# The first weights of a hybrid decoder layer in two parts of 256 columns, and half of x's first tile by ScalarE's queue

## The chip, the cores and the metric

The kernel runs on one core of a Trainium2 chip. The metric is the device time of one execution in microseconds (us). Before the change three runs took 457.81, 458.18 and 458.72 us; the median is 458.18.

A core has five engines with a queue of instructions each, and they work side by side: TensorE (PE in the profile; PEld is its weight load) for matmuls, VectorE (DVE) and ScalarE (ACT) for arithmetic on tiles, GpSimd (POOL), and SyncE (SP), which here issues most of the transfers from memory. ScalarE can issue transfers too, in the order of its own instructions. Engines wait for each other and for transfers by semaphores.

## The reference

One layer of a hybrid decoder: a normalised input goes through one wide projection; its columns feed a block-sparse attention, a gated linear recurrence and two merge gates. The part of it that matters here is the first:

```python
def rmsnorm(x, gain):
    xf = x.astype(jnp.float32)
    return xf * lax.rsqrt(jnp.mean(xf * xf, axis=-1, keepdims=True) + RMS_EPS) * gain.astype(jnp.float32)
...
    xn = rmsnorm(h, norm_gain[i]).astype(dt)
    proj = xn @ w_in[i]
    aq, ak, av, ag, bq, bf, bi, bg, gate_a, gate_b = jnp.split(proj, split_pts, axis=-1)
```

x is 512 tokens by 1024 features, `w_in` is 1024 by 6144, all in float32. `bi` (the recurrence's values) and `av` (the attention's values) are 512 columns each, and are the first two projections that the kernel computes.

## The kernel before

Every float32 product is made of three matmuls in a faster type, `fp32r`. Both operands are split into a high part (a copy in the narrower type) and a low part (the rest): `gh`, `gl` for x times its gain, `wh`, `wl` for a weight. Then high times high, low times high and high times low are summed in PSUM. For a tile of x the high part is made by ScalarE (`A.activation`, with the gain as scale) and the low part by VectorE. For weights it is the same, except the very first one, whose high part VectorE casts, since ScalarE is taken by x there.

x lies transposed: eight tiles `xr0` to `xr7` of 128 features by 512 tokens. The projections `bi` and `av` are computed with tokens in the partitions: four PSUM banks each, one for 128 tokens. `chunk(g, k, ts)` adds the product of feature tile k into the banks `ts` of `bi` (g = 2) or `av` (g = 3): for each of the three products one matmul of 512 columns per bank. The factor of the norm (one number per token) is put on later, so that these matmuls can start before the sum of squares is known.

The order of instructions on ScalarE, VectorE and SyncE in this first stretch, and on TensorE throughout, is the order in which the code calls them. It begins so:

- TensorE runs eight matmuls on constants (`warm`, L156) while the first data come.
- SyncE issues, in this order: the left half of `xr0` (tokens 0 to 255), the first half of the first weights `wf0` (128 features by 512 columns, 256 KB), the right half of `xr0`, the first half of `wf1` (for `av`), `xr1`, and the second halves of `wf0` and `wf1` (L283 to L289). ScalarE's queue brings only `sm`, the small vectors with the gain (L141, 9 KB).
- `w_halves(0)` and `w_halves(1)` are generators that split the weights half by half, one step at each `next`. The first step casts the first half of `wf0` on VectorE (L312).
- Then x's left half is scaled and split (L205, L206), `chunk(2, 0, (0, 1))` multiplies it for the token banks 0 and 1, x's right half is scaled and split, and `chunk(2, 0, (2, 3))` follows. Then come `chunk(3, 0)` with `wf1`, and so on with the next tiles of x.
- A one-element `memset` on VectorE (L852) holds the transfer of `xr2` back until VectorE has come that far.

Of the kernel before, what the change touches and what calls it, by code (L numbers as in the profile page):

```python
# [11 lines left out]
F32 = mybir.dt.float32  # L12
R = mybir.dt.float32r
I32 = mybir.dt.int32
AF = mybir.ActivationFunctionType
OP = mybir.AluOpType
# [44 lines left out]
def hybrid_layer_kernel(  # L61
# [15 lines left out]
    nc = tc.nc  # L77
    V, A, G, PE = nc.vector, nc.scalar, nc.gpsimd, nc.tensor
# [11 lines left out]
    def unit(tag, name, dt=F32, shape=(128, 512)):  # L90
        return sb.tile(list(shape), dt, tag=tag, bufs=BUFS[tag], name=name)

    def bank(tag, name):
        return psum.tile([128, 512], F32, tag=tag, bufs={"mm": 4, "g": 2, "a": 2}[tag], name=name)
# [15 lines left out]
    def spawn(gen, after=0.0):  # L110
        sides.append([now[0] + after, gen])

    def run_due():
        again = True
        while again:
            again = False
            for s_ in list(sides):
                w = s_[0]
                if callable(w):
                    if not w():  # L120
                        continue
                elif w > now[0]:
                    continue
                again = True
                try:
                    y = next(s_[1])
                    s_[0] = y if callable(y) else now[0] + y
                except StopIteration:
                    sides.remove(s_)

    def tick(us):
        now[0] += us
        run_due()
# [3 lines left out]


    sm = cst.tile([128, NSMALL], F32, name="sm")
    with tc.high_priority():  # L140
        nc.scalar.dma_start(sm, smalls)  # L141
    A.preload_act_table_set("natural_log_exp_and_others")
    mkf = cst.tile([128, 32 + 32 * 7], F32, name="mkf")
    xr = []

    def load_x(k0, k1):
        for k in range(k0, k1):
            t = unit("H", f"xr{k}")
            nc.sync.dma_start(t, xT[:, k, :])
            xr.append(t)  # L150
# [18 lines left out]
    gain = sm[:, 0:8]  # L169
# [9 lines left out]
    def lower_bound():  # L179
        V.tensor_scalar(qgain, sm[:, 8:9], 0.125, None, op0=OP.mult)  # L180
        V.tensor_copy(lb[:, 0], lbl)
        V.tensor_sub(lb[:, 1], lbl, lb[:, 0])
        A.activation(lb[:, 1], lb[:, 1], AF.Exp)
        V.reciprocal(lb[:, 2], lb[:, 1])
        V.tensor_mul(lb[:, 2], lb[:, 1], lb[:, 2])
        V.tensor_sub(lb[:, 3], lb[:, 2], lb[:, 2])
        V.tensor_scalar(lb[:, 4], lb[:, 3], -1.0, 1.0, op0=OP.mult, op1=OP.add)
        A.activation(lb[:, 5], lb[:, 4], AF.Ln)
# [11 lines left out]
    def split(hi, lo, src):  # L200
        A.activation(hi, src, AF.Copy)
        V.tensor_tensor(lo, src, hi.bitcast(F32), op=OP.subtract)

    def scale_split(hi, lo, src, g):
        A.activation(hi, src, AF.Copy, scale=g)  # L205
        V.scalar_tensor_tensor(lo, src, g, hi.bitcast(F32), op0=OP.mult, op1=OP.subtract)  # L206

    wseq, wraw, wtile, wpos = [], [], [], [0]
# [19 lines left out]
    def w_load(upto):  # L228
        while len(wraw) <= min(upto, len(wseq) - 1):
            ap, kn, cols = wseq[len(wraw)]  # L230
            raw = unit("w", f"wf{len(wraw)}", shape=(128, kn, cols))
            nc.sync.dma_start(raw, ap)
            wraw.append(raw)

    def w_split(upto):
        while len(wtile) <= min(upto, len(wseq) - 1):
            i = len(wtile)
            w_load(i)
            ap, kn, cols = wseq[i]
            hi = unit("wh", f"wh{i}", R, (128, kn, cols))  # L240
            lo = unit("wl", f"wl{i}", R, (128, kn, cols))
            with tc.high_priority(offset=AHEAD):
                A.activation(hi, wraw[i], AF.Copy)  # L243
                pin(V.tensor_tensor(lo, wraw[i], hi.bitcast(F32), op=OP.subtract))  # L244
            wtile.append((hi, lo))
# [31 lines left out]


    with tc.high_priority():
        x0 = unit("H", "xr0")  # L280
        xr.append(x0)
        wraw.extend(unit("w", f"wf{i}", shape=(128, 2, 512)) for i in range(2))
        nc.sync.dma_start(x0[:, 0:256], xT[:, 0, 0:256])  # L283
        nc.sync.dma_start(wraw[0][:, 0], wseq[0][0][:, 0])
        nc.sync.dma_start(x0[:, 256:512], xT[:, 0, 256:512])
        nc.sync.dma_start(wraw[1][:, 0], wseq[1][0][:, 0])
        load_x(1, 2)
        for i in range(2):
            nc.sync.dma_start(wraw[i][:, 1], wseq[i][0][:, 1])  # L289


    gh, gl, xh, xl = [], [], [], []
# [3 lines left out]
    def x_gain(k0, k1):  # L296
        for k in range(k0, k1):
            h_ = unit("A", f"gh{k}", R)
            l_ = unit("A", f"gl{k}", R)
            scale_split(h_, l_, xr[k], gain[:, k:k + 1])  # L300
            gh.append(h_)
            gl.append(l_)

    def w_halves(i):

        hi = unit("wh", f"wh{i}", R, (128, 2, 512))
        lo = unit("wl", f"wl{i}", R, (128, 2, 512))
        wtile.append((hi, lo))
        for kk in range(2):
            if i == 0 and kk == 0:  # L310

                V.tensor_copy(hi[:, kk], wraw[i][:, kk])  # L312
                yield
                V.tensor_tensor(lo[:, kk], wraw[i][:, kk], hi[:, kk].bitcast(F32), op=OP.subtract)
            else:
                split(hi[:, kk], lo[:, kk], wraw[i][:, kk])
            yield
# [3 lines left out]
    def x_square(k):  # L321
        if k == 0:
            A.activation(ssum, xr[0], AF.Square)
            return
        t = unit("YB", f"xsq{k}")
        A.activation(t, xr[k], AF.Square)
        V.tensor_tensor(ssum, ssum, t, op=OP.add)
# [21 lines left out]
    def x_norm():  # L349
        with tc.high_priority(offset=AHEAD):  # L350
            y, rstd = column_norms(ssum, D, "xn", "YB")
            for g in range(4):
                V.tensor_copy(rt[32 * g:32 * g + 32], y[0:32].rearrange("p (t g) -> p t g", g=4)[:, :, g])
            x_normalise(rstd)
        done.add("rt")
        yield RT
# [468 lines left out]

    tok = {2: [bank("mm", f"bi{t}") for t in range(NT)], 3: [bank("ga"[t // 2], f"av{t}") for t in range(NT)]}

    def chunk(g, k, ts=range(NT)):

        wh, wl = wtile[PAIRED.index((g, k // 2))]  # L830
        for x_, w_, i in ((gh, wh, 0), (gl, wh, 1), (gh, wl, 2)):
            for t in ts:
                PE.matmul(tok[g][t], x_[k][:, t * 128:t * 128 + 128], w_[:, k % 2, :], start=(k == 0 and i == 0),  # L833
                          stop=(k == KD - 1 and i == 2))
            tick(0.227 * len(ts))
# [3 lines left out]
    with tc.manual_schedule(engines=FIRST):  # L839
        h_ = unit("A", "gh0", R)  # L840
        l_ = unit("A", "gl0", R)
        gh.append(h_)
        gl.append(l_)
        w0, w1 = w_halves(0), w_halves(1)
        next(w0)
        scale_split(h_[:, 0:256], l_[:, 0:256], xr[0][:, 0:256], gain[:, 0:1])
        next(w0)
        chunk(2, 0, (0, 1))
        scale_split(h_[:, 256:512], l_[:, 256:512], xr[0][:, 256:512], gain[:, 0:1])
        chunk(2, 0, (2, 3))  # L850
        t = unit("H", "xr2")
        V.memset(t[:, 0:1], 0.0)  # L852
        nc.sync.dma_start(t, xT[:, 2, :])
        xr.append(t)
        load_x(3, 4)
        next(w1)
        chunk(3, 0)
        x_gain(1, 2)
        next(w0)
        chunk(2, 1)  # L860
        w_load(2)
        load_x(4, 5)
        next(w1)
        chunk(3, 1)
        w_load(3)
        load_x(5, KD)
        x_square(0)
        x_square(1)
        x_gain(2, 3)
        w_split(2)  # L870
        x_gain(3, 4)
        chunk(2, 2)
        chunk(2, 3)
        x_square(2)
        w_load(4)
        w_split(3)
        x_square(3)
        x_gain(4, 5)
        x_square(4)
        w_load(5)  # L880
        chunk(3, 2)
        x_gain(5, 6)
        x_square(5)
        chunk(3, 3)
        x_square(6)
        x_gain(6, 7)
        x_square(7)
        w_split(4)
        x_gain(7, KD)
        lower_bound()  # L890
        nc.sync.dma_start(mkf, masks)
        wpos[0] = 4
        spawn(x_norm())
# [48 lines left out]
    for n in range(KD):  # L942
# [3 lines left out]
        h_ = unit("YB", f"mh{n}", R)  # L946
        l_ = unit("A", f"ml{n}", R)
# [140 lines left out]
    for at, n in enumerate(PAIRS):  # L1088
# [24 lines left out]
        if at in (2, 3):  # L1113
            t = unit("A", f"pf{at}")
# [201 lines left out]
```

## Time and profile before

| what | value |
|---|---|
| median of three runs | 458.18 us (457.81 to 458.72) |
| the profiled execution | 458.14 us |
| its span, first to last instruction | 456.1 us |
| TensorE busy | 450.5 us, 99% |
| VectorE busy | 338.7 us, 74% |
| ScalarE busy | 290.6 us, 64% |
| TensorE's granted clock over the span | 1.0 |
| bytes moved by DMA | 57.80 MB, 127 GB/s on average |

The span is counted from the first instruction to the last; the execution's own time is 2.0 us longer. In the profile `wf<-in_w_tok_dram` is a transfer of weights, `xr<-in_xT_dram` one of x; `wh`, `wl`, `gh` and `gl` are the split parts, and `bi` and `av` PSUM banks. In a timeline each line has the start and the length in us, the engine, the line of the kernel, the operation, what it writes and reads, and in brackets how long the engine stood idle before it and what ended that. SPq and ACTq are the issues of transfers on SyncE's and ScalarE's queues. A line of the view of waits has who waited for whom, then us in total, how many times, and the longest. In a group of instructions the numbers are us busy and mean ns of one.

### The profile page before, as it was taken

The numbers are of one execution on the slowest core, as the hardware profiler recorded it, in microseconds if no ns is written. First come the engines' busy times: TensorE is split into PE (matmuls) and PEld (weight loads), VectorE is DVE, ScalarE is ACT, GpSimd is POOL, SyncE is SP. The second block draws the span as 40 slices with busy tenths as digits, with TensorE's granted clock in tenths as the row PEclk, the third lists the DMA queues.
The fourth block names the chain that finished last, engine by engine and source line by source line (L and its number), as shares of the span: only waits on it lengthen the run. The fifth ranks groups of instructions, "written<-read, shape, count | busy, mean of one in ns | idle before, by whom it ended". The sixth has DMA issues, their size and how long they took to land.

```text
span 456.1 us, 7786 instructions
## 1 busy us (share of the span) xinstructions
PE 450.5 (99%) x2903; PEld 383.9 (84%) x2903; DVE 338.7 (74%) x718; ACT 290.6 (64%) x534; POOL 9.0 (2%) x32
## 2 busy tenths in 40 slices
PE   8999999999999999999999999999999999999996
PEld 7888888888888888888888888888888888899996
DVE  5789567869989778958798456414368878899885
ACT  5837555658688988889799487666224445457431
POOL 1000000010000010001000100000000000000000
PEclk9999999999999999999999999999999999999999
DMA  6742223342744344244424442224324534463112
GB/s 212 262 139 92 94 92 99 116 157 65 242 133 143 104 149 147 87 126 140 167 71 144 122 156 93 82 70 136 107 70 119 203 100 161 155 208 116 48 47 93
DMA packets 24358, 57.80 MB, mean 127 GB/s; under 512 B 2944, under 2 KB 5888, under 8 KB 24320
## 3 DMA queue, kind: packets, MB, share of 16 engines
q1 hardware_dynamic: 19568, 49.95, 34.5%
q10 hardware_dynamic: 4752, 7.35, 4.4%
q8 instruction: 23, 0.38, 0.3%
q14 instruction: 15, 0.12, 0.1%
HBM read 45.75 MB, written 2.10 MB: 105 GB/s over the span
## 4 chain that ended last, share of the span: by engine, by line
PE 98%; DMA 1%; DVE 0%; ACT 0%; issue 0%; SPq 0%; ACTq 0%; DVEq 0%
PE gb L260 10%; PE ga L260 10%; PE h L260 10%; PE ak L388 5%; PE ub L260 5%; PE bq L260 5%; PE bi L833 5%; PE bf L260 5%; PE ag L260 5%; PE aq L388 5%; PE bg L260 5%; PE av L833 5%; PE ua L260 5%; PE pe L1143 2%; PE gc L1152 2%; PE gd L1152 2%
## 5 line engine op out<-in xcount | busy, mean ns | idle before, releaser
L243 ACT ACTIVATE wh<-wf 128x1024 fp32r<-128x1024 f32 (+1 forms) x70 | 67.2, 960 | 66.9 <-PE ub L260 10.8
L244 DVE TENSOR_TENSOR wl<-wf,wh 128x1024 fp32r<-128x1024 f32 (+1 forms) x70 | 76.9, 1099 | 39.5 <-ACT wh L243 37.9
L260 PE MATMUL gb<-xh,wh 128*128 128x512 f32 x64 | 25.7, 402 | 0.0
L260 PE MATMUL ga<-xh,wh 128*128 128x512 f32 x64 | 25.2, 393 | 0.0
L260 PE MATMUL gb<-xh,wl 128*128 128x512 f32 x64 | 25.0, 391 | 0.0
L260 PE MATMUL ga<-xh,wl 128*128 128x512 f32 x64 | 25.0, 390 | 0.0
L260 PE MATMUL ga<-xl,wh 128*128 128x512 f32 x64 | 25.0, 390 | 0.0
L260 PE MATMUL gb<-xl,wh 128*128 128x512 f32 x64 | 25.0, 390 | 0.0
L260 PE MATMUL h<-ml,wh 128*128 128x512 f32 x64 | 24.9, 389 | 0.0
L260 PE MATMUL h<-mh,wl 128*128 128x512 f32 x64 | 24.9, 389 | 0.0
L260 PE MATMUL h<-mh,wh 128*128 128x512 f32 x64 | 24.9, 389 | 0.0
L708 ACT ACTIVATE p<-p,ps 128x128 f32<-128x128 f32 (+3 forms) x32 | 17.6, 552 | 5.5 <-DVE ps L706 5.5
L706 DVE CUSTOM_DVE_ANT_0 p<-s,bias 128x128 f32<-128x128 f32 (+3 forms) x32 | 14.2, 485 | 5.9 <-PE s L697 4.5
L718 ACT ACTIVATE p<-p,ps 128x128 f32<-128x128 f32 (+3 forms) x32 | 15.9, 552 | 0.5 <-DVE ps L716 0.5
L260 PEld LDWEIGHTS gb<-xh,wl 128*128 128x128 f32 x64 | 12.0, 188 | 2.6
L260 PEld LDWEIGHTS ga<-xh,wl 128*128 128x128 f32 x64 | 12.0, 188 | 2.6
L260 PEld LDWEIGHTS h<-mh,wh 128*128 128x128 f32 x64 | 12.0, 188 | 2.5
L260 PEld LDWEIGHTS h<-ml,wh 128*128 128x128 f32 x64 | 12.0, 188 | 2.5
L260 PEld LDWEIGHTS h<-mh,wl 128*128 128x128 f32 x64 | 12.0, 188 | 2.4
L260 PEld LDWEIGHTS ga<-xl,wh 128*128 128x128 f32 x64 | 12.0, 188 | 2.3
L260 PEld LDWEIGHTS ga<-xh,wh 128*128 128x128 f32 x64 | 12.0, 188 | 2.3
L260 PEld LDWEIGHTS gb<-xl,wh 128*128 128x128 f32 x64 | 12.0, 188 | 2.2
(408 smaller groups left out, 1368.5 us busy)
## 6 DMA issues: line engine op xcount, KB each, us to landing
wf<-in_w_tr_dram SPq DMA_DIRECT2D x32, 512.0 KB, 3.3
wf<-in_w_tok_dram SPq DMA_DIRECT2D x14, 512.0 KB, 3.3
wf<-in_w_up_dram SPq DMA_DIRECT2D x16, 256.0 KB, 2.7
wf<-in_w_o_dram SPq DMA_DIRECT2D x8, 512.0 KB, 3.3
pc<-p ACTq DMA_DIRECT2D x16, 192.0 KB, 2.2
bias<-in_brow_dram SPq DMA_DIRECT2D x8, 256.0 KB, 3.4
pc<-p ACTq DMA_DIRECT2D x8, 256.0 KB, 2.7
xres<-in_xT_dram SPq DMA_DIRECT2D x8, 256.0 KB, 3.0
```

What stands on the lines that cost most here:

```text
L243: A.activation(hi, wraw[i], AF.Copy)
L244: pin(V.tensor_tensor(lo, wraw[i], hi.bitcast(F32), op=OP.subtract))
L260: PE.matmul(ps, a[:, k, :], b[k], start=(n == 0), stop=(n == tot - 1))
L388: PE.matmul(banks[t], a[:, s_], b[:, kk, :], start=(k == 0 and i == 0), stop=(k == KD - 1 and i == 2))
L706: V.tensor_tensor_reduce(p_, sp[j][:, o:o + nk], T[2 * hp + j][:, nk - 1::-1], -1.0, 3e38, OP.add, OP.min, st[:, 0:1])
L708: A.activation(p_, p_, AF.Exp, bias=st[:, 0:1], scale=-1.0, accum_out=st[:, 1:2])
L718: A.activation(p_, p_, AF.Copy, scale=st[:, 2:3])
L833: PE.matmul(tok[g][t], x_[k][:, t * 128:t * 128 + 128], w_[:, k % 2, :], start=(k == 0 and i == 0), stop=(k == KD - 1 and i == 2))
L1143: PE.matmul(pes[i][:, cols], wt[:, i, k, :], t[k][:, cols], start=k == n == 0, stop=k == 1 and n == 2 and (bool(parts) or cols == right))
L1152: PE.matmul(dst[:, left], wt[:, k, :], bt, start=begin and n == 0, stop=n == 11, skip_group_check=not begin)
```

## The change

Three things change at the start of the program:

- x's right half is issued on ScalarE's queue, behind `sm`, instead of on SyncE's.
- The first half of `wf0` comes in two transfers of 256 columns. VectorE casts the left one, and ScalarE copies the right one into its high part. VectorE makes the two low parts one after the other.
- The products of token banks 0 and 1 with these weights are made by a new function, `first_chunk`, in matmuls of 256 columns: left columns and then right columns in each of the three products.

The steps of x's left half are written out, so that they stand between the steps of the weights. The rest of the program is the same.

```diff
+    x0 = unit("H", "xr0")
     with tc.high_priority():
         nc.scalar.dma_start(sm, smalls)
+        nc.scalar.dma_start(x0[:, 256:512], xT[:, 0, 256:512])
...
         nc.sync.dma_start(x0[:, 0:256], xT[:, 0, 0:256])
-        nc.sync.dma_start(wraw[0][:, 0], wseq[0][0][:, 0])
-        nc.sync.dma_start(x0[:, 256:512], xT[:, 0, 256:512])
+        for cols in (slice(0, 256), slice(256, 512)):
+            nc.sync.dma_start(wraw[0][:, 0, cols], wseq[0][0][:, 0, cols])
         nc.sync.dma_start(wraw[1][:, 0], wseq[1][0][:, 0])
...
             if i == 0 and kk == 0:
-
-                V.tensor_copy(hi[:, kk], wraw[i][:, kk])
+                l_, r_ = slice(0, 256), slice(256, 512)
+                V.tensor_copy(hi[:, kk, l_], wraw[i][:, kk, l_])
                 yield
-                V.tensor_tensor(lo[:, kk], wraw[i][:, kk], hi[:, kk].bitcast(F32), op=OP.subtract)
+                A.activation(hi[:, kk, r_], wraw[i][:, kk, r_], AF.Copy)
+                yield
+                for cols in (l_, r_):
+                    V.tensor_tensor(lo[:, kk, cols], wraw[i][:, kk, cols], hi[:, kk, cols].bitcast(F32), op=OP.subtract)
...
+    def first_chunk():
+
+        wh, wl = wtile[0]
+        for n, (x_, w_) in enumerate(((gh, wh), (gl, wh), (gh, wl))):
+            for cols in (slice(0, 256), slice(256, 512)):
+                for t in (0, 1):
+                    PE.matmul(tok[2][t][:, cols], x_[0][:, t * 128:t * 128 + 128], w_[:, 0, cols],
+                              start=(n == 0 and cols.start == 0), stop=False)
+        tick(0.227 * 6)
...
-        scale_split(h_[:, 0:256], l_[:, 0:256], xr[0][:, 0:256], gain[:, 0:1])
+        A.activation(h_[:, 0:256], xr[0][:, 0:256], AF.Copy, scale=gain[:, 0:1])
         next(w0)
-        chunk(2, 0, (0, 1))
+        V.scalar_tensor_tensor(l_[:, 0:256], xr[0][:, 0:256], gain[:, 0:1], h_[:, 0:256].bitcast(F32),
+                               op0=OP.mult, op1=OP.subtract)
+        next(w0)
+        first_chunk()
```

SyncE's queue at the start of the program, before the change and then after it (`xr0` is x's first tile, `wf0` and `wf1` the first two weights):

```order
L283 DMA xr0_94<-in_xT_dram 128x256
L284 DMA wf0_95<-in_w_tok_dram 128x512
L285 DMA xr0_94<-in_xT_dram 128x256
L286 DMA wf1_96<-in_w_tok_dram 128x512
L149 DMA xr1_101<-in_xT_dram 128x512
```

```order
L284 DMA xr0_67<-in_xT_dram 128x256
L286 DMA wf0_96<-in_w_tok_dram 128x256 x2
L287 DMA wf1_97<-in_w_tok_dram 128x512
L151 DMA xr1_102<-in_xT_dram 128x512
L290 DMA wf0_96<-in_w_tok_dram 128x512
```

Four transfers stand ahead of `xr1` in both (`x2` counts two). The 256 KB of `wf0` are now two of 128 KB, and x's second 128 KB are no longer among them.

ScalarE's queue at the same place, before and after (`gh0` is x's high part, `wh0` and `wh1` those of the weights):

```order
L141 DMA sm_66<-in_smalls_dram 128x18
L142 ACT_TABLE_LOAD
L205 ACTIVATE gh0_120<-xr0_94,sm_66 128x256 x2
L201 ACTIVATE wh1_147<-wf1_96 128x512
L205 ACTIVATE gh1_163<-xr1_101,sm_66 128x512
```

```order
L142 DMA sm_66<-in_smalls_dram 128x18
L143 DMA xr0_67<-in_xT_dram 128x256
L144 ACT_TABLE_LOAD
L860 ACTIVATE gh0_121<-xr0_67,sm_66 128x256
L315 ACTIVATE wh0_123<-wf0_96 128x256
L207 ACTIVATE gh0_121<-xr0_67,sm_66 128x256
L203 ACTIVATE wh1_156<-wf1_97 128x512
```

The issue of x's right half stands ahead of the table load, and the copy of the weights' right half stands between the two scalings of x.

TensorE's queue behind the warm matmuls, before and after (`bi0` and `bi1` are the banks of tokens 0 to 127 and 128 to 255, `bi2` the next):

```order
L833 MATMUL bi0_110<-wh0_122,gh0_120 128x512
L833 MATMUL bi1_111<-wh0_122,gh0_120 128x512
L833 MATMUL bi0_110<-wh0_122,gl0_121 128x512
L833 MATMUL bi1_111<-wh0_122,gl0_121 128x512
L833 MATMUL bi0_110<-wl0_123,gh0_120 128x512
L833 MATMUL bi1_111<-wl0_123,gh0_120 128x512
L833 MATMUL bi2_112<-wh0_122,gh0_120 128x512
```

```order
L838 MATMUL bi0_111<-wh0_123,gh0_121 128x256
L838 MATMUL bi1_112<-wh0_123,gh0_121 128x256
L838 MATMUL bi0_111<-wh0_123,gh0_121 128x256
L838 MATMUL bi1_112<-wh0_123,gh0_121 128x256
L838 MATMUL bi0_111<-wh0_123,gl0_122 128x256
L838 MATMUL bi1_112<-wh0_123,gl0_122 128x256
```

Six matmuls have become twelve of half the width; of these the first two read only the left columns of the weights, and the third and fourth the right ones.

More of the change, by code (lines that the diff above doesn't have):

```diff
@@ L279, in hybrid_layer_kernel @@
     with tc.high_priority():
-        x0 = unit("H", "xr0")
         xr.append(x0)
```

## The prediction

> **What bounds the kernel now.** I read the head of the page first, then the chain of work that ended last.
>
> ```profile
> span 456.1 us, 7786 instructions
> PE 450.5 (99%) x2903; PEld 383.9 (84%) x2903; DVE 338.7 (74%) x718; ACT 290.6 (64%) x534; POOL 9.0 (2%) x32
> PE 98%; DMA 1%; DVE 0%; ACT 0%; issue 0%; SPq 0%; ACTq 0%; DVEq 0%
> ```
>
> TensorE (PE) is busy for 99% of the span and makes 98% of the chain. No other engine can pay for a saved microsecond; only idle time of PE on that chain can. The view of waits, for PE alone over the whole span, shows how much of that there is:
>
> ```profile
> PE bi L833 <- DVE wh L312: 1.0, 1, 1.0
> PE warm L156 <- PEq L1303: 0.8, 1, 0.8
> PE ktp L670 <- ACT sc L548: 0.4, 1, 0.4
> ```
>
> Three waits. The 0.8 us is the program's start and the 0.4 us belongs to the attention; the change touches neither. What is left is one wait of 1.0 us, ahead of the first real matmul. The timeline around it, thinned to what matters:
>
> ```profile
> 0.73 0.39 SPq L283 DMA_DIRECT2D xr<-in_xT_dram  x1
> 0.74 0.41 ACTq L141 DMA_DIRECT2D sm<-in_smalls_dram  x1
> 1.18 0.42 SPq L284 DMA_DIRECT2D wf<-in_w_tok_dram  x1
> 1.19 1.28 ACT L142 ACT_TABLE_LOAD   x1 [1.19 <-PEq L1303]
> 1.65 0.42 SPq L285 DMA_DIRECT2D xr<-in_xT_dram  x1
> 2.11 0.43 SPq L286 DMA_DIRECT2D wf<-in_w_tok_dram  x1
> 3.23 0.51 ACT L205 ACTIVATE gh<-xr,sm 128x256 fp32r<-128x256 f32 x1 [0.76 <-DMA sm<-in_smalls_dram]
> 3.75 0.38 PE L156 MATMUL warm<-const-float32-1.0 128*128 128x128 f32 x2
> 4.53 0.43 DVE L312 CAST wh<-wf 128x512 fp32r<-128x512 f32 x1 [3.64 <-DMA wf<-in_w_tok_dram]
> 4.93 0.51 ACT L205 ACTIVATE gh<-xr,sm 128x256 fp32r<-128x256 f32 x1 [1.20 <-DMA xr<-in_xT_dram]
> 5.11 0.70 PE L833 MATMUL bi<-wh,gh 128*128 128x512 f32 x2 [0.98 <-DVE wh L312]
> 5.27 0.69 DVE L314 TENSOR_TENSOR wl<-wf,wh 128x512 fp32r<-128x512 f32 x1
> 6.44 0.63 ACT L201 ACTIVATE wh<-wf 128x512 fp32r<-128x512 f32 x1 [0.99 <-DMA wf<-in_w_tok_dram]
> 6.58 0.63 PE L833 MATMUL bi<-wh,gh 128*128 128x512 f32 x2
> 7.96 1.08 PE L833 MATMUL av<-wh,gh 128*128 128x512 f32 x4
> ```
>
> The warm matmuls end at 3.75 + 0.38 = 4.13. The first weights land, VectorE (DVE) casts them from 4.53 to 4.96, and PE starts at 5.11. x's left part and its scaling are done by 3.74, so the weights alone decide. From 5.11 on PE has work at every moment but that 0.4 us. So **the whole of what can be won is 5.11 - 4.13 = 0.98 us**, 0.21% of 458.14. The time can fall by over 0.2% (0.92 us, about what a measurement of this kernel can tell from no change) only if nearly all of it is won.
>
> When the transfers land, from the view of DMAs cut to the moment of each issue (last column: us from issue to landing):
>
> ```profile
> xr<-in_xT_dram SPq DMA_DIRECT2D x1, 128.0 KB, 2.3
> wf<-in_w_tok_dram SPq DMA_DIRECT2D x1, 256.0 KB, 3.3
> xr<-in_xT_dram SPq DMA_DIRECT2D x1, 128.0 KB, 3.3
> wf<-in_w_tok_dram SPq DMA_DIRECT2D x1, 256.0 KB, 4.3
> ```
>
> With the issue times above that is 3.03 for 128 KB in all, 4.48 for 384 KB, 4.95 for 512 KB and 6.41 for 768 KB. I use these four marks below: what SyncE's queue had brought by when.
>
> **The change part by part.** Two things move: x's right part (128 KB) goes from SyncE's queue to ScalarE's, and the first 256 KB of weights become two halves of 128 KB, the left cast by DVE and the right by ScalarE (ACT). SyncE still issues four transfers up to the second weights, so those are issued at 2.11 as before.
>
> *The left half* lands at a time L. Before it come x's left part and perhaps some of x's right part: between the 256 KB mark, which an even share of 3.03 to 4.48 puts at 3.75, and the 384 KB mark, 4.48. The cast of 256 columns has no row; half of the 0.43 above and all of it bound it, and I take 0.30. Pick-up (4.48 to 4.53) is 0.05 and cast to PE (4.96 to 5.11) is 0.15. PE starts at L + 0.50, from 4.25 to 4.98: 0.1 to 0.9 earlier. If that were all, the change would be a gain. But the left half feeds two matmuls, and the third needs the right half.
>
> *The right half* lands at R. ACT copies it; the nearest rows are a copy of this size, and the scaled one of the same size:
>
> ```profile
> L966 ACT ACTIVATE b11h<-hf 128x256 fp32r<-128x256 f32 x3 | 1.2, 402 | 0.0
> L205 ACT ACTIVATE gh<-xr,sm 128x256 fp32r<-128x256 f32 x2 | 1.0, 510 | 2.0 <-DMA xr<-in_xT_dram 1.2 <-DMA sm<-in_smalls_dram 0.8
> ```
>
> So 0.40 to 0.51; I take 0.41, the plain copy. ACT to PE has no row at such a place; I take DVE's 0.15, with 0.03 as the other end (ACT to DVE, 7.07 to 7.10). The third matmul starts at R + 0.05 + 0.41 + 0.15 = **R + 0.61**.
>
> *The matmuls.* Six of 512 columns become twelve of 256. From the stretch near the end of the kernel, where 24 matmuls of that size stand between these two:
>
> ```profile
> 405.07 0.29 PE L1152 MATMUL ga<-b11h,gwh 128*128 128x256 f32 x1
> 407.87 0.28 PE L1152 MATMUL gc<-tah,s1h 128*128 128x256 f32 x1
> ```
>
> 2.80 / 24 = 0.117 each, 1.40 for twelve, against 1.47 from 5.11 to 6.58 now (it includes a short wait for `wl`). Ten are left when the right half is ready, 1.17 us. **The next pair of tiles starts at R + 1.78, against 6.58 now. The change breaks even at R = 4.80.**
>
> *So what is R?* By then x's left part, both halves and some share of x's right part have come: at least 384 KB and at most 512 KB. The marks give 4.48 (-0.32 us) and 4.95 (+0.15 us). Nothing in the trace shows two queues loading from memory together: `sm` on ACT's queue is 9 KB. Since x's right part is issued at about 1.15, ahead of the right half (1.65), most of it should be in front; since it is behind `sm`, not all. I take R = 4.80, nearer the upper mark: **0.0 us**. PE's wait is then cut in two: it starts at about 4.6, does 0.23 us of work, and stands again until about 5.4.
>
> [...]
>
> *What hides the rest.* ACT issues one more DMA, 0.41 us, ahead of its table load, which then ends at about 2.88 instead of 2.47; the first ACTIVATE waits for `sm` until 3.23 anyway. Without that cover it would cost nothing until PE's 4.25. On ACT the wait for the right half now stands ahead of x's right scaling (0.51), which ends at R + 0.97 and is needed at R + 1.78; behind it ACT has the second weights at 6.44, later than both. On DVE the right `wl` is done at about R + 0.9 and needed at R + 1.55. Each margin is 0.6 to 0.8 us; past it each costs one for one.
>
> *Whether a gain would last.* The second weights' high part is ready at 6.44 + 0.63 + 0.15 = 7.22 against its use at 7.96: 0.74 of the 0.98 us passes, unless those weights come sooner too. After that:
>
> ```profile
> 12.59 1.06 ACT L243 ACTIVATE wh<-wf 128x1024 fp32r<-128x1024 f32 x1 [1.89 <-DMA wf<-in_w_tok_dram]
> 16.13 1.07 PE L833 MATMUL bi<-wh,gh 128*128 128x512 f32 x4
> 47.33 1.29 DVE L202 TENSOR_TENSOR xl<-xr,xh 128x512 fp32r<-128x512 f32 x2
> 48.77 0.39 PE L260 MATMUL bf<-xh,wh 128*128 128x512 f32 x1
> ```
>
> The third weights are ready at 13.65 for 16.13, and the last of `xl` at 48.62 for a use 21 matmuls behind 48.77. So whatever the start gains or loses, up to 0.74 us, goes to the end unchanged.
>
> **The rivals.** *Faster: R comes early.* The rate over 40 slices of 0.7 to 4.6 us:
>
> ```profile
> GB/s 0 0 0 0 0 0 0 0 0 0 21 95 126 127 192 265 271 297 284 282 341 420 399 420 273 200 179 147 126 137 105 126 95 74 105 158 221 158 189 168
> ```
>
> It reaches 420 near 3 us and sags to about 130 until past 4. Nothing I can name causes the sag. If two queues fill it, 384 KB behind the 3.03 mark at 400 GB/s take 0.98: R = 4.01, a gain of 0.79, of which 0.74 passes: 457.4. Against it: the sag falls when SyncE's queue already holds enough work. 25%.
>
> *Slower: the right half falls behind.* The marks at 512 and 768 KB are 1.46 us apart, so a late mark is as much in the trace as an early one. If the sag meets R, halfway between them, R = 5.68; PE stands in the middle of its first chunk with everything queued behind it, and loses 0.88: 459.0. It decides from R = 4.80 on, one for one. Against it: it needs more than the 512 KB to be served ahead. 10%.
>
> *The change does not do what it says:* x's right part is served ahead of the left half, L is 4.48 and R 4.95; PE starts 0.13 sooner, and the next pair 0.15 later: 458.3. 5%.
>
> **How the numbers follow.** The sum is made against the profiled execution: 458.14 us, of which 456.1 are its span and 2.0 lie around it. The median of the three runs, 458.18, is the same; they lie 0.91 apart. Forecast, no change, 60%: 458.1. Of the faster case's 25%, 8 end over 0.92 us faster with that scatter, and of the forecast's 60 about 2; of the slower case's 10%, 4 end over 0.92 us slower, and about 2 of the forecast's. Faster 10%, same 84%, slower 6%. The range runs from the faster case with a little scatter, 457.3, to just short of the slower case, 458.9.
>
> **What would show it.** In the profile after: PE's first real matmul between 4.25 and 5.0, then two matmuls of 256 columns, then a second wait whose releaser is ACT's `wh`. The twelve take 1.4 us without their wait. ACT's copy of the right half starts near 4.85 and takes 0.4. The pair of tiles 2 and 3 starts within 0.3 us of 6.58, and every later chunk keeps that shift. The prediction is wrong if the copy starts before 4.5 or after 5.2, or if a wait of PE stands anywhere later that was not there before.

## The result, and the profile after

The changed kernel takes 461.28 us (median of 21 runs, 458.73 to 463.21) against 458.37 us (457.40 to 459.04) for the kernel before in the same measurement. The ratio is **1.0061, 95% interval 1.0050 to 1.0071**: about 2.8 us slower. The prediction was 458.1 us, no change.

The runs of the changed kernel do not lie around one value: five are below 460 us and sixteen between 460.7 and 463.2.

The head of the page of the changed kernel, its chain, and the transfers of code, which are a queue of their own:

```profile
span 459.2 us, 7803 instructions
PE 453.4 (99%) x2909; PEld 386.4 (84%) x2909; DVE 338.8 (74%) x719; ACT 290.6 (63%) x535; POOL 10.0 (2%) x32
q8 instruction: 23, 0.38, 0.3%
PE 98%; DMA 1%; issue 0%; DVE 0%; SPq 0%; ACT 0%; DVEq 0%
```

PE still makes 98% of the chain, and it is busy 2.9 us longer, though it has only six matmul records more (2909 against 2903). The waits of PE over the whole span:

```profile
PE pt L741 <- issue: 0.8, 1, 0.8
PE warm L158 <- PEq L1320: 0.8, 1, 0.8
PE bi L838 <- ACT wh L315: 0.5, 1, 0.5
```

The wait of 1.0 us has become one of 0.5 us, so the start looks better. A wait at `pt` is new. Neither explains 3 us. The timeline of the start does:

```profile
1.18 0.89 SPq L286 DMA_DIRECT2D wf<-in_w_tok_dram  x2
1.18 0.44 ACTq L143 DMA_DIRECT2D xr<-in_xT_dram  x1
4.02 0.29 DVE L313 CAST wh<-wf 128x256 fp32r<-128x256 f32 x1 [3.13 <-DMA wf<-in_w_tok_dram]
4.46 0.77 PE L838 MATMUL bi<-wh,gh 128*128 128x256 f32 x2
5.25 0.42 ACT L315 ACTIVATE wh<-wf 128x256 fp32r<-128x256 f32 x1 [1.53 <-DMA wf<-in_w_tok_dram]
5.72 0.80 PE L838 MATMUL bi<-wh,gh 128*128 128x256 f32 x2 [0.49 <-ACT wh L315]
6.32 1.05 PE L838 MATMUL bi<-wh,gl 128*128 128x256 f32 x4
8.02 1.05 PE L847 MATMUL bi<-wh,gh 128*128 128x512 f32 x2
8.88 1.05 PE L847 MATMUL bi<-wh,gl 128*128 128x512 f32 x2
9.73 0.75 PE L847 MATMUL bi<-wl,gh 128*128 128x512 f32 x2
10.32 1.09 PE L847 MATMUL av<-wh,gh 128*128 128x512 f32 x4
11.25 1.08 PE L847 MATMUL av<-wh,gl 128*128 128x512 f32 x4
```

PE starts at 4.46 instead of 5.11 and is ahead. But read the distance from row to row: two matmuls of 512 columns take 8.88 - 8.02 = 0.86 us, 0.43 each; four take 11.25 - 10.32 = 0.93, 0.23 each. **TensorE runs at half rate until about 10 us.** In the kernel before it had full rate from its first real matmul on: the six from 6.58 to 7.96 in the prediction's rows take 0.23 us each. The trace also keeps a record of each change of the granted clock, with its time, and that says the same: full rate from 9.98 here, from 3.57 before. `av` starts at 10.32 against 7.96, so 2.36 of the span's 3.0 us are lost by then.

The right half came late too. The view of DMAs cut to the issues at 1.2 to 1.7 us (the right half of the weights is issued near 1.6):

```profile
xr<-in_xT_dram ACTq DMA_DIRECT2D x1, 128.0 KB, 3.7
wf<-in_w_tok_dram SPq DMA_DIRECT2D x1, 128.0 KB, 3.6
```

ScalarE takes the right half up at 5.25, so R was 5.20 where the prediction had 4.80.

### The profile page after: what moved, and what is told of

Same layout as the page of the kernel before. It is cut to its first block, busy times and chain, and to the rows that moved or that the text cites. A ratio compares the mean times of both kernels' runs of the same rounds, so it can differ in the third digit from the quotient of the medians.

```text
span 459.2 us, 7803 instructions
## 1 busy us (share of the span) xinstructions
PE 453.4 (99%) x2909; PEld 386.4 (84%) x2909; DVE 338.8 (74%) x719; ACT 290.6 (63%) x535; POOL 10.0 (2%) x32
## 4 chain that ended last, share of the span: by engine, by line
PE 98%; DMA 1%; issue 0%; DVE 0%; SPq 0%; ACT 0%; DVEq 0%
PE gb L262 10%; PE ga L262 10%; PE h L262 10%; PE ak L392 5%; PE ub L262 5%; PE bq L262 5%; PE bf L262 5%; PE ag L262 5%; PE aq L392 5%; PE bg L262 5%; PE av L847 5%; PE ua L262 5%; PE bi L847 5%; PE pe L1160 2%; PE gc L1169 2%; PE gd L1169 2%
```

## The experiments

Three causes had to be told apart: the clock, the late landing through the second queue, and something later in the program, where the wait at `pt` is. Ratios are to the kernel before, run beside each kernel on the same chip. The kernels were run in four sets, not all on one chip, so I compare medians only within a set, and otherwise the ratios.

**First set: fill the pauses, undo the queue, move the queue alone, lengthen the pause.**

Filling TensorE's pauses of the changed kernel:

```diff
-WARM = 8
+WARM = 9
...
             for cols in (slice(0, 256), slice(256, 512)):
+                if n == 0 and cols.start:
+                    for i in range(3):
+                        PE.matmul(tok[2][2][:, 0:128], one, one, start=True, stop=True)
                 for t in (0, 1):
```

> The changed kernel with one more warm matmul at the start and three matmuls on constants (into a bank that is overwritten later) in the wait between the second and the third real matmul: the pauses of TensorE are filled, nothing else moves. Clock theory: what the change costs is mostly TensorE at half rate until about 10 us (512 columns in 0.43 us instead of 0.23), because the two pauses keep it from full speed; filled, full rate comes before 7 us and the time is 457.9 to 459.0 us, ratio 0.999 to 1.001. Landing theory: the right half of the weights and its copy on ScalarE come late and the delay is passed on; filling does nothing, the time stays at 460.5 to 461.5 us, ratio 1.005 to 1.007.

Measured 460.05 us, ratio 1.0039 (1.0027 to 1.0052): between the two. The trace shows why. The copy of the right half started at 5.14, nearly as late as in the changed kernel, but the rate was full:

```profile
5.61 0.51 PE L841 MATMUL bi<-wh,gh 128*128 128x256 f32 x2
5.96 0.64 PE L841 MATMUL bi<-wh,gl 128*128 128x256 f32 x4
6.43 0.64 PE L841 MATMUL bi<-wl,gh 128*128 128x256 f32 x4
6.91 0.63 PE L850 MATMUL bi<-wh,gh 128*128 128x512 f32 x2
```

Four matmuls of 256 columns in 0.47 us, and the next pair at 6.91, 0.33 late instead of 1.44 (8.02). With full rate most of the loss at the start is gone. The trace alone does not show that filling brought it: its clock record has full rate from 4.04, ahead of the filled wait. The times say more: all five runs lie between 459.90 and 461.02, where sixteen of the changed kernel's twenty-one were over 460.7, although this kernel loses 1.2 us between 200 and 260 us, 0.9 more than the changed one. Neither theory had that. In its waits there is a new 1.1 us, and two lines of the timeline show it between dense small matmuls:

```profile
253.31 0.46 PE L541 MATMUL lpa<-hq,hk 128*32 128x48 f32 x24
254.83 0.29 PE L541 MATMUL lpa<-hq,hk 128*32 128x48 f32 x8 [1.06 <-issue]
```

PE waited for nothing that the profile shows ("issue"), in the middle of a series. I come back to it.

x's right half back on SyncE's queue, the split kept:

```diff
-        nc.scalar.dma_start(x0[:, 256:512], xT[:, 0, 256:512])
...
+        nc.sync.dma_start(x0[:, 256:512], xT[:, 0, 256:512])
         nc.sync.dma_start(wraw[1][:, 0], wseq[1][0][:, 0])
```

> The changed kernel with x's right half back on SyncE's queue, behind both halves of the weights: only the queue move is undone. Landing theory: the right half lands at the 384 KB mark, near 4.5 us, the copy on ScalarE starts near 4.5 instead of 5.25, and the time is at or a little below before, ratio 0.999 to 1.000. [...]

Measured 458.85 us, ratio 1.0007 (0.9998 to 1.0015). The timeline of its PE:

```profile
4.18 1.10 PE L838 MATMUL bi<-wh,gh 128*128 128x256 f32 x4
5.12 0.64 PE L838 MATMUL bi<-wh,gl 128*128 128x256 f32 x4
5.59 0.64 PE L838 MATMUL bi<-wl,gh 128*128 128x256 f32 x4
6.07 0.63 PE L847 MATMUL bi<-wh,gh 128*128 128x512 f32 x2
```

The cast began at 3.58 and ScalarE's copy at 4.18, a microsecond sooner than in the changed kernel. The pair of tiles 2 and 3 starts at 6.07, 0.51 ahead of before. So on one queue the split does what it was drawn up to do. The gain of 0.5 us is then gone again by the end of the span (456.1 us, as before): 0.2 of it near 254 us, where PE waits at `pt` here too, and 0.2 behind the last matmul.

Only the queue moved, no split:

```diff
         nc.scalar.dma_start(sm, smalls)
+        nc.scalar.dma_start(x0[:, 256:512], xT[:, 0, 256:512])
...
-        nc.sync.dma_start(x0[:, 256:512], xT[:, 0, 256:512])
```

> The kernel before with only x's right half moved to ScalarE's queue; the weights come, are cast and are multiplied whole. Landing theory: the weights now share the engines with x's right half, the cast starts near 4.9 to 5.2 instead of 4.53, cost 0.3 to 0.7 us, ratio 1.001. Clock theory: one pause of 1.3 to 1.6 us instead of 1.0, so full rate can be missed as in the changed kernel: then 460 to 462 us, ratio 1.004 to 1.007, and half rate past 8 us in the trace.

Measured 461.19 us, ratio 1.0060 (1.0044 to 1.0077): **the move of one transfer to the other queue makes the whole loss by itself.** Its PE:

```profile
6.70 0.91 PE L833 MATMUL bi<-wh,gh 128*128 128x512 f32 x2 [2.55 <-DVE wh L312]
7.40 1.05 PE L833 MATMUL bi<-wh,gl 128*128 128x512 f32 x2
8.25 1.05 PE L833 MATMUL bi<-wl,gh 128*128 128x512 f32 x2
9.11 1.05 PE L833 MATMUL bi<-wh,gh 128*128 128x512 f32 x2
```

The weights landed at 6.08 instead of 4.48 and x's right half, issued at 1.19, took 5.1 us. That is later than either theory had, and then comes half rate. The clock record of this trace has full rate from 3.61, half from 7.02 and full again from 10.43: half rate came 0.32 us behind the wait of 2.55 us.

Four warm matmuls instead of eight in the kernel before (`WARM = 4`):

> The kernel before with four warm matmuls instead of eight: nothing but the pause ahead of the first real matmul changes, from 1.0 to about 2.6 us. Landing theory: the first weights decide when TensorE starts, so the time is that of before, ratio 0.999 to 1.001. [...]

Measured 459.54 us, ratio 1.0021 (1.0012 to 1.0030). Half rate went on behind PE's first wait, 1.89 us instead of 0.98, and the time is over that of before, which the landing theory did not have:

```profile
4.71 1.19 PE L833 MATMUL bi<-wh,gh 128*128 128x512 f32 x2 [1.89 <-DVE wh L312]
5.70 1.05 PE L833 MATMUL bi<-wh,gl 128*128 128x512 f32 x2
6.56 1.05 PE L833 MATMUL bi<-wl,gh 128*128 128x512 f32 x2
7.41 0.96 PE L833 MATMUL bi<-wh,gh 128*128 128x512 f32 x2
8.21 0.63 PE L833 MATMUL bi<-wh,gl 128*128 128x512 f32 x2
```

PE starts 0.40 sooner (the weights happened to land sooner) and `av` starts at 9.13, 1.17 later; full rate came at 8.12. Near 254 us this kernel wins 0.6 us back: the wait that the kernel before has there is gone. It has eight matmul records fewer (2895).

**Second set: the stream of code.** Across these traces the time near 254 us goes with the number of matmuls ahead of it: 0.6 us won with 2895 records, 0.2 to 0.3 lost with 2909, and 1.2 lost with 2917 (there with the stall near 206 us). The warm matmuls can be made fewer without less time:

```diff
-    for i in range(WARM):
-        PE.matmul(warm[:, 0:128], one, one, start=True, stop=True)
+    wide = nc.const_aps.tensor(1.0, (128, 512), F32)
+    for i in range(2):
+        PE.matmul(warm, one, wide, start=True, stop=True)
```

> The kernel before with its eight warm matmuls of 128 columns written as two of 512: the same columns, so the same warm time, but six matmul instructions fewer ahead of everything else. Code theory: where in TensorE's stream its code runs out depends on how many instructions stand ahead, and six more of them in the changed kernel cost 0.3 to 0.5 us at the dense small matmuls near 254 us; six fewer than before win 0.3 to 0.5 us there, 457.9 us, ratio 0.999. Without that theory: no change, ratio 0.9995 to 1.0005, and the same 0.4 us wait near 254 us.

Measured 457.58 us, ratio 0.9984 (0.9974 to 0.9994), as that theory had it. Its PE near 254 us runs through, where the kernel before waits:

```profile
252.45 0.55 PE L538 MATMUL lpa<-hq,hk 128*32 128x48 f32 x32
252.93 0.71 PE L738 MATMUL pt<-identr,pc 128*128 128x128 f32 x6
253.47 0.50 PE L671 MATMUL ktp<-identr,kc 128*128 128x128 f32 x4
```

`ktp` starts here at 253.47, there at 254.03, while 20 us earlier both stand at the same time. Six matmul instructions (twelve records) are the only difference.

The same two wide warm matmuls in the changed kernel:

> The changed kernel with the same two wide warm matmuls, so with as many matmul instructions as before. Code theory: the loss at the start stays (2 to 3 us by the first matmuls of av, with half rate until then), and the 0.4 to 0.5 us lost later goes: 460.8 us, ratio 1.0045 to 1.0055. Without that theory: 461.2 us as the changed kernel, ratio 1.006.

Measured 458.75 us, ratio 1.0022 (1.0002 to 1.0041), but its twelve runs go from 457.81 to 462.08. The part behind 200 us came out as expected (0.74 us late before that place, 0.16 behind it). The start did not: its profiled run, of 458.70 us, had full rate from 4.51 on, and nine of the twelve runs are below 460 us, where five of the changed kernel's twenty-one were. I had not expected that, and comparing it with the changed kernel needed both on one chip (fourth set).

The changed kernel filled, with wide warm matmuls (two, one of 128 columns, and one of 384 in the second pause):

> The changed kernel with both: wide warm matmuls, one of 128 columns more, and one of 384 columns in the second pause; two matmul instructions more than before instead of ten. Clock theory with code theory: full rate before 7 us, start late by 0.2 to 0.6 us, and the stalls near 206 and 254 us back to about 0.4 us: 458.5 to 459.1 us, ratio 1.000 to 1.0015. Clock theory alone: 460.0 us as with the first filling, ratio 1.004.

Measured 459.55 us, ratio 1.0024 (1.0013 to 1.0034), over what was expected. The rate was full from 3.69 on and no run exceeds 460.01, but ScalarE's copy began only at 6.02, and `ktp` waits 0.4 us again. Late landing alone costs 1.2 us in this trace.

The wide warm matmuls with the split on one queue:

> The changed kernel with x's right half back on SyncE's queue and the two wide warm matmuls. Queue theory: one queue brings the right half near 4.1 instead of 5.2 us, so the second pause is short, the clock is not missed, and the start is 0.4 to 0.6 us sooner than before; with code theory nothing is lost later: 457.8 us, ratio 0.9985 to 0.9995. Without code theory 458.7 us as the split alone, ratio 1.0005.

Measured 457.76 us, ratio 0.9987 (0.9977 to 0.9997), as expected. It is not faster than the kernel before with the same warm matmuls (457.58 in the same set): the split itself wins nothing that can be measured.

**Third set.** Halves of 256 columns for the first product only:

```diff
-            for cols in (slice(0, 256), slice(256, 512)):
+            for cols in ((slice(0, 256), slice(256, 512)) if n == 0 else (slice(0, 512),)):
```

> A version meant to be faster than both: two wide warm matmuls, x's right half on SyncE's queue behind both halves of the weights, and only the first of the three products in halves of 256 columns (the other two have both halves by then), so eight matmuls in the first chunk instead of twelve. Code theory: four matmul instructions fewer than the wide-warm split; the stall near 254 us stays away: 457.4 to 457.8 us, ratio 0.998 to 0.9995. If the whole split is worth nothing, it equals the kernel before with wide warm matmuls, 457.6 us, ratio 0.9984.

Measured 457.71 us, ratio 0.9985 (0.9976 to 0.9993): the same again.

The wide-warm split without warming up (one matmul of 16 columns):

> The wide-warm split with its two warm matmuls cut to one of 16 columns: landing, queue order and the stream of code stay as they are (one matmul instruction less), only TensorE has done nothing before the first weights. [...] Without the clock theory 457.7 us, ratio 0.9987.

Measured 458.56 us, ratio 1.0012 (1.0003 to 1.0022), against 457.71 in the same set. The direction is that of the clock theory; the size is 0.85 us at the median. Four of the eleven runs are at 459.6 to 460.2, seven at 458.4 to 458.9. The profiled run, of 459.62 us, had the halves as early as ever (cast at 3.58, copy at 4.26) and half rate until 9.69:

```profile
4.02 1.50 PE L838 MATMUL bi<-wh,gh 128*128 128x256 f32 x4 [2.67 <-DVE wh L313]
5.32 1.05 PE L838 MATMUL bi<-wh,gl 128*128 128x256 f32 x4
6.18 1.05 PE L838 MATMUL bi<-wl,gh 128*128 128x256 f32 x4
9.59 1.14 PE L847 MATMUL av<-wh,gh 128*128 128x512 f32 x4
```

With one queue and early weights, `av` is 1.6 us late here against the kernel before, by the clock alone; this run is one of the four above 459.6.

The queue moved alone, but the issue written behind the table load:

> The kernel before with x's right half on ScalarE's queue, but issued behind the table load (near 2.5 us instead of 1.2). Contention theory: the first weights are served before it comes, so the cast starts at 4.0 to 4.6 as before; x's right half lands at 5.3 to 6.3, just in time or up to 0.4 us late; ratio 0.999 to 1.0015. If a second queue delays the weights whenever it is used, the cast starts after 5 us again and the time is 460 to 461.5 us, ratio 1.004 to 1.0065, as with the early issue.

Measured 460.47 us, ratio 1.0045 (1.0026 to 1.0065), twelve runs from 458.18 to 463.10. The edit did not do what I meant: the issue still went out at 1.22, beside the table load, so this is the move alone once more. It taught something else. The profiled run, of 458.32 us, had the cast at 4.39 and x's right half at 4.75, as early as on one queue. **The second queue makes the landing erratic rather than always late.**

**Fourth set: the changed kernel and three forms of it on one chip.** The changed kernel with three wide warm matmuls had run alone before:

> The changed kernel with three wide warm matmuls; against the run with two (458.75 us median, 457.8 to 462.1) nothing else moves. TensorE is then busy until 5.1 to 5.9 us, so the pauses of about 0.6 and 0.4 us in front of the two halves of the weights shrink or go. Clock theory: half rate past 7 us no longer happens, and the runs at 460 to 462 us go: 458.0 to 459.2 us median with none over 460, ratio 1.000 to 1.0015; what is left above the split on one queue (457.7) is the late landing. If the long tail stays, the landing itself makes it, not the clock.

Measured 458.91 us, ratio 1.0015 (1.0006 to 1.0024), no run over 459.83, as the clock theory said. Then side by side, the changed kernel, two wide, three wide and twelve narrow warm matmuls:

> The changed kernel itself once more, beside the three below on one chip. Both theories: 460.5 to 462 us median, ratio 1.005 to 1.007, most of its runs over 460.5 us.

> Two wide warm matmuls instead of eight narrow ones, same warm time. If chips don't differ: 458.7 us median with a tail to 462, ratio 1.002, that is 2 us under the changed kernel though its pauses are the same. If the earlier gap was a difference of chips: 460 to 461 us, only the 0.5 us of the stalls behind 200 us less.

> Three wide warm matmuls, so TensorE is busy until 5.1 to 5.9 us. Clock theory: no run over 460.2 us, median 458.3 to 459.3, at or under the kernel with two, whatever that one does. Landing theory: it is no faster than the kernel with two and has the same tail.

> The changed kernel with twelve narrow warm matmuls instead of eight: busy until 4.9 to 5.9 us, four matmul instructions more. Clock theory: the runs over 461 go; with the stalls of more code behind 200 us (as with the first filling) 459.3 to 460.2 us, ratio 1.002 to 1.004, so 1 to 2 us under the changed kernel. Landing theory: as slow as the changed kernel or slower.

| kernel | median us | runs from .. to | ratio (95%) |
|---|---|---|---|
| changed kernel | 460.98 | 459.32 .. 461.50 | 1.0047 (1.0031 to 1.0064) |
| two wide warm matmuls | 458.44 | 457.69 .. 461.80 | 1.0021 (1.0001 to 1.0041) |
| three wide warm matmuls | 458.87 | 457.89 .. 460.03 | 1.0013 (1.0002 to 1.0023) |
| twelve narrow warm matmuls | 460.14 | 459.47 .. 460.82 | 1.0043 (1.0027 to 1.0058) |

With two wide ones seven runs are at 457.7 to 458.5 and five at 460.3 to 461.8, with nothing between; with three the upper group is gone, as the clock theory said and the landing theory did not. So I put that gap of two to three microseconds down to the clock; no run of the upper group was profiled. The median with three is 0.4 over that with two, against my expectation. In the two profiles with three, the first real matmul started 0.2 and 0.3 us after its weights were ready, behind the warm ones; whether that makes the 0.4 was not tested. Twelve narrow ones bring no run over 460.82, but they carry more code; their gain of 0.8 us at the median cannot be told from nothing with six and seven runs. The difference between the kernels with eight narrow and two wide warm matmuls is no difference of chips: on one chip it is 2.5 us, of which the place near 254 us makes 0.8 (0.2 lost there with eight narrow ones, 0.6 won with two wide ones).

## Why the prediction was wrong

*What bounds the kernel, and the 0.98 us that could be won:* right for the start; PE still makes 98% of the chain. The other 0.4 us of waiting, near 254 us, could be won too: two wide warm matmuls win it in the kernel before.

*The left half:* right. PE started at 4.46, inside 4.25 to 4.98, did two matmuls, and waited for ScalarE's `wh` as said.

*The right half:* the copy took 0.42 us (0.41 taken) and the third matmul came 0.47 after the copy's start (0.56 taken). R was 5.20, and 5.57 in the second profile of the changed kernel, over both ends of the range, 4.48 and 4.95. Both ends are marks that SyncE's queue had set alone. In ten of the eleven profiles with x's right half on ScalarE's queue the last of the first weights were taken up at 5.1 to 6.1; in the seven without it, at 3.9 to 4.5. By the prediction's own sum these two R cost 0.40 and 0.77 us.

*The matmuls, "0.117 each", and "it decides from R = 4.80 on, one for one":* **this is the step that failed.** The 0.117 was read where TensorE has full rate, and in the changed kernel it does not have it: the ten matmuls left from the third on took 8.02 - 5.72 = 2.30 us, not 1.17. At full rate the pair of tiles 2 and 3 would have started at 6.98 and 7.35. `av` was late by 2.36 and 2.42 us instead of 0.40 and 0.77, so half rate took 1.96 and 1.65 us. The first filling bears the sum out at full rate: there R was 5.10, R + 1.78 is 6.88, and the pair started at 6.91. The sign of half rate was there before the change: in the kernel before the warm matmuls' records start 0.21 us apart until 3.47 and 0.11 apart from 3.63 on, so the rate doubled between, and the prediction did not ask what it hung on.

What full rate hangs on is not shown: the trace has the changes of the clock, not what brought them. The same eight warm matmuls run from 0.77 on in both kernels, and up to 3.46 the starts of their records agree within 0.01 us. Then they come 0.11 apart in the kernel before, and stay 0.21 apart in the changed kernel to the last one, at 4.10. So TensorE's work up to there does not by itself decide when full rate comes.

The runs show that long waits ahead of the first real matmul went with half rate: 1.89 us with four warm matmuls (until 8.12), 2.67 without warming up (until 9.69), 2.55 with the queue alone moved (from 7.02 to 10.43). Waits of 0.3 to 0.6 us went with either: half rate in the two profiles of the changed kernel (one of 0.49; 0.50 and 0.30), full rate from 4.51 with two wide warm matmuls (0.63 and 0.35). The wait of 0.98 in the kernel before left the rate full. So I take it that the same code can have full rate early in one execution and not in the next. That fits runs in two groups; no trace of both groups of one kernel was taken to show it.

*"Whatever the start gains or loses goes to the end unchanged":* wrong by 0.2 to 0.3 us near 254 us in the two profiles of the changed kernel. The last wait, 0.4 us at `ktp`, was put down to ScalarE and to the attention, and "the change touches neither". It moves with the amount of code ahead of it. The shift against the kernel before changes there by -0.6 us with 2891 to 2897 matmul records (seven profiles), by -0.5 and -0.2 with 2899, by 0.0 to +0.2 with 2901 and 2903, by +0.2 to +0.3 with 2909, and by +0.4 and +1.2, the stall near 206 us included, with 2917. In the changed kernel that is this row, behind a wait of 0.77:

```profile
256.18 0.71 PE L741 MATMUL pt<-identr,pc 128*128 128x128 f32 x6 [0.77 <-issue]
```

In every trace with such a wait a block of code of 16 KB has landed 1.2 to 1.5 us before the wait ends. That PE waits for that code is inferred from this and from the shift with the number of records; the profile does not name it. The blocks are in the traces (23 of them, 0.38 MB, in the line of the page above), and the stretch is dense: in the kernel before PE goes through 96 matmuls of 48 columns in 1.2 us there.

*The rivals:* the slower one was the nearest, with the right mechanism for the smaller part of the loss (0.40 and 0.77 us). None had a change of rate. The sum that holds for the two profiles of the changed kernel is: landing 0.4 to 0.8, half rate 1.7 to 2.0, the wait near 254 us 0.2 to 0.3; the spans are 3.0 and 2.9 us longer. Of the rest 0.2 lies at the end: from the start of the last matmul to the end of the span it is 3.8 us in the five profiles without the split and 4.0 us in the thirteen with it. Why is open.

*The prediction's own signs:* two came that it had named. The copy began at 5.25, after 5.2, and a wait stood at `pt` that was not there before. Neither was the half rate that made most of the loss.

*Still open:* what brings TensorE to full rate, and why a second queue delays the first transfers. The longest packet on it before 6.5 us took 0.9 to 2.2 us in the eleven traces with the move; on SyncE's queue alone the longest took 0.7 to 1.3 us in the seven without. What holds them was not tried. Nor is it settled why the changed kernel stays below 460 us more often with two wide warm matmuls (16 of 24 runs) than with eight narrow ones of as many columns (8 of 28).

A version that beats both is the kernel before with two wide warm matmuls: ratio 0.9984 (0.9974 to 0.9994). It has no part of the change.

## What to carry to other kernels

A pause of TensorE near the start can cost more than its length: with four warm matmuls PE waited 1.89 us instead of 0.98, started 0.40 sooner, ran at half rate until 8.12, and `av` came 1.17 later. Compare the time per matmul before and behind a pause, and fill it or close it. The transfers that the start waits for landed best here on the one queue that brings the rest of the start, where the last of the first weights was taken up at 3.9 to 4.5 us; moving another transfer beside them to a second queue bought nothing and made that 4.4 to 6.1. And an edit that changes only the number of instructions can move a wait hundreds of microseconds later (0.6 us near 254 us, with twelve matmul records fewer at the start), so a wait that the profile puts down to a neighbour in a dense stretch should be tested with a few instructions more or fewer.

## What the runs showed of the hardware that was not expected

- The mean granted clock hides half rate at the start: the view of cores gives 1.000 for the second profile of the changed kernel, which ran at half rate until 9.70 us. The clock record begins with its first change, and the mean counts what lies ahead of it as full: 1.00 for 4.2 to 6.0 us of the changed kernel, where the first record is at 9.98. The time per matmul shows it (0.43 against 0.23 us for 512 columns).

```profile
core 0: 459.0 us, clock 1.000
```

- ScalarE's table load, 1.28 us, did not hold back the issue of a transfer written behind it: with the load from 1.19 the issue went out at 1.22.
- Twelve matmul records fewer, with as many warm columns, made the kernel 0.16% faster (0.06 to 0.26%).
